# Late modulation vectors as float32 products on TensorE, and six of sixteen gate blocks issued beside the attention's first four query blocks

## Chip, cores and metric

One core of one Trainium2 chip. The metric is the device time of one execution in microseconds (us). The engines are named TensorE (PE in the rows; PEld is its weight load), VectorE (DVE), ScalarE (ACT), GpSimd (POOL) and SyncE (SP). L1035 is line 1035 of the kernel.

## The reference, cut to what matters

The reference is one layer of a hybrid block over 1024 tokens of width 1024. What bears on this change:

```python
mod_x = silu(c) @ w_mod + b_mod              # (1, 6*1024), float32
sh1, sc1, g1, sh2, sc2, g2 = split(mod_x, 6)
hx = layer_norm(x) * (1 + sc1) + sh1
q, k, v, u_hy, gate_x = split(hx @ w_in)     # gate_x has 2048 columns
att = window_attention(q, k, v, k_ctx, v_ctx, sink)
hy = hyena(u_hy, ...)                        # short convolution, then two long ones
g_att, g_hy = split(sigmoid(gate_x), 2)
y = (g_att * (att @ w_ba) + g_hy * (hy @ w_bh)) @ w_o
x_mid = layer_norm(ALPHA * x + g1 * y, ln1_g, ln1_b)
h = layer_norm(x_mid) * (1 + sc2) + sh2
out = layer_norm(ALPHA * x_mid + g2 * moe(h), ln2_g, ln2_b)
```

The first two modulation vectors (sh1, sc1) are needed at the start. The other four, the late ones, are needed after the attention: g1 for the output projection, sh2 and sc2 for the second norm, g2 in the experts.

## The kernel before, in words

The kernel runs in stages: the Hyena filters and the normed input (to about 230 us), the two long convolutions with the projections beside them (230 to 634 us), the attention's query blocks 0 to 3 (634 to 745), blocks 4 to 7 with the first half of the merge beside them (745 to 853), the rest of the merge and the output projection, and from about 1000 us the experts, whose weights stream from memory to the end.

Every projection of the normed input (`proj`, products on L812) handles 128 output columns as a block: a weight block of 1024x128 is loaded on SP's queue (tile `wr`), split into two float16 parts by ScalarE (`wh`, L791) and VectorE (`wl`, L799), and multiplied in 2 halves of 512 tokens by 24 products each. A gate block (`gate(j)`, j from 0 to 15) passes the result through a sigmoid on ScalarE (L841) into a tile `t` and stores it to DRAM (`Gd[j]`) from ScalarE's queue; the merge loads it back. The first eight gate blocks belong to the attention's branch, the last eight to the Hyena's.

The long convolution (`hyena(hf, o, z)`) runs four times, for two halves of the channels and two orders. Each run transposes on TensorE, transforms by products (L899, then the inverse on L922), and does radix-8 butterflies on VectorE (L722, L747, L748, L763, L906 to L909, tile `bf`); it ends with z products on VectorE (L924, L926).

Late modulation (`mod_late`) makes each late vector on VectorE: for each of eight chunks of 128 input rows it loads 128x1024 of `w_mod` on ScalarE's queue (L1034) and does one multiply-add over 128x1024 into an accumulator (L1035). Products with a column of ones then sum over the partitions (16 for g2 on L1039, two halves for each of the others on L1047). The tile size t4 (five buffers) is shared by these loads, the accumulator, uconv's outputs and the gates' results.

Order: the code is generators that yield, and `mix(M, (F, k))` issues k steps of F for each step of M. Issue order sets the priority, `hp` raises it (the hyena's by 1000 or 1500, the weight splits and the projections' copies out of PSUM by 3000); a scheduler then lists the instructions of each engine by its own estimate of time, and each engine runs its list in order. Before, all sixteen gate blocks are issued beside the hyena and drained (`GD=1`), and then the attention begins. PSUM has three buffers `mm` (projections, attention scores for the maximum, merge), three `ff` (the transforms, attention scores for the exponential) and two `tp` (transposes, modulation, attention output).

The attention (`attn`, L975 to L1010) computes scores for the row maximum (L975, L976; the maximum on L977 and L978), scores again in the other orientation (L991 to L994), two exponentials on ScalarE (L996, L997), and the product with V (L1004 to L1006). After block 3 the space of the normed input and of the projections is given to the merge: the branch weights (`wb_load`, L1062 load, L1063 split, tile `big`) go there.

Of the kernel before, what the change touches and what calls it, by code (L numbers as in the profile page):

```python
# [13 lines left out]
F32 = mybir.dt.float32  # L14
# [4 lines left out]
AF = mybir.ActivationFunctionType  # L19
ALU = mybir.AluOpType  # L20
# [74 lines left out]
class Moe:  # L95
# [144 lines left out]
    def prep_(s,C,p,pos,M,res,G0=None,late=None):  # L240

        nc,wk,ps=s.nc,s.wk,s.ps
        n=-(-C//128); chunks=[]; G={}; st={}
        def one():

            for i in range(min(n,2) if late is None else 1): hot(i)
# [9 lines left out]
        def gather(i):  # L256
# [13 lines left out]
            else:  # L270
# [4 lines left out]
                late.append(f); s.order.append(csi.ins)  # L275
            g=G[i]=G0[i] if G0 is not None else wk.tile([128,2,D],F16,name="g%d"%p,bufs=2)
            nc.gpsimd.indirect_dma_start(out=g[:cs].rearrange("p a d -> p (a d)"),out_offset=None,in_=s.rows,in_offset=bass.IndirectOffsetOnAxis(ap=gi[:cs,:1],axis=0))  # L277
            chunks.append((c0,cs,si,gc))
        def tr(i):

            if i==0:
                st['x']=wk.tile([128,2,8,PMAX[p]],F16,name="xT%d"%p,bufs=1); res.append((st['x'],chunks))
            c0=i*128; cs=min(128,C-c0); g=G.pop(i)
            for q in range(2):
# [153 lines left out]
    def experts(s,only=None):  # L438
# [14 lines left out]
        s.tail=[]; ready=[[],[]]; preps=[None,None]; run=[None,None]; done=[0,0]  # L453
        def nextprep(l,G=None,late=None):
            preps[l]=s.prep(seq[l][done[l]],l,ready[l],G,late) if done[l]<len(seq[l]) else None
            if preps[l] and G is None: preps[l][0].append(lambda r=seq[l][done[l]]: s.brs.__setitem__(s.regs[r],s.bias_load(s.regs[r]())))
            done[l]+=1
# [480 lines left out]
class PhaseA2(PhaseA):  # L938
# [86 lines left out]
    def mod_late(s):  # L1025

        nc,A=s.nc,s.A
        for n,nm in ((5,'g2'),(2,'g1'),(3,'sh2'),(4,'sc2')):
            acc=s.t4()
            nc.gpsimd.memset(acc,0.0)  # L1030
            if nm!='g2': nc.scalar.dma_start(acc[0:1],A['b_mod'][0:1,n*1024:(n+1)*1024])
            for k in range(8):
                w=s.t4()
                nc.scalar.dma_start(w,A['w_mod'][k*128:(k+1)*128,n*1024:(n+1)*1024])  # L1034
                (nc.gpsimd if s.poolm else nc.vector).scalar_tensor_tensor(acc,w,s.S[:,0,k:k+1],acc,op0=ALU.mult,op1=ALU.add)  # L1035
                yield
            if nm=='g2':
                p=s.ptp()[:,:8]
                for j in range(8): nc.tensor.matmul(p[:,j:j+1],acc[:,j*128:(j+1)*128],s.ones32[:,0:1],start=True,stop=True)  # L1039
                s.g2c=s.mcp.tile([128,8],F32,name="g2c"); s.g2s=s.mcp.tile([128,8],F32,name="g2s")  # L1040
                nc.vector.tensor_tensor(s.g2c,p,s.cols[:,88:96],op=ALU.add)
                nc.vector.tensor_scalar(s.g2s,s.g2c,2.**-10/ALPHA,None,op0=ALU.mult)
                nc.vector.tensor_scalar(s.g2c,s.g2c,1.0/ALPHA,None,op0=ALU.mult)
            else:
                r=acc
                for h in range(2):
                    p=s.ptp()[0:1]; nc.tensor.matmul(p,s.ones32[:,0:1],acc[:,h*512:(h+1)*512],start=True,stop=True)  # L1047
                    sc,bi={'g1':(1.0,0.0),'sc2':(1.0,1.0),'sh2':(1.0,0.0)}[nm]
                    nc.scalar.activation(r[0:1,h*512:(h+1)*512],p,AF.Copy,scale=sc,bias=bi)
                nc.sync.dma_start(s.rowD[n-2:n-1],r[0:1])  # L1050
            yield
    poolm=False

# [139 lines left out]
        c+=k  # L1193
        while c>=1: next(M,None); c-=1
SK=2
GD=1
HP0,HP1=1000,1500
def skew(gens,lag):

# [5 lines left out]
def drain(*gs):  # L1205
    for g in gs:
        for _ in g: pass
def chain(*gs):
    for g in gs: yield from g
# [7 lines left out]
def build(nc,tc,A,out,dbg=None,nexp=32):  # L1217
    with ExitStack() as es:
# [3 lines left out]
        with ExitStack() as ea:  # L1222
# [47 lines left out]
            F=chain(*[a.uconv(8+c,a.zt[c]) for c in range(4)],*[a.uconv(j) for j in range(4)])  # L1270
# [7 lines left out]
            drain(F)  # L1278
            nc.sync.dma_start(a.dft2,dq('idft')); a.idft=a.dft2
            F=chain(*[a.uconv(4+j) for j in range(4)],a.vproj(),*[a.qk(wq,j) for j in (4,0,1,2,3)])  # L1280
            G=chain(F,*[a.gate(j) for j in range(16)])
            ML=a.mod_late()
            mix(hp(chain(a.hyena(0,0,a.zt[0:2]),a.hyena(1,0,a.zt[2:4])),HP0),(G,K2),(ML,KM))
            drain(F)
# [2 lines left out]
            a.nq2=1; a.attn_k(w0); a.attn_q(0)  # L1287
            mix(hp(chain(a.hyena(0,1,a.zt[0:2]),a.hyena(1,1,a.zt[2:4])),HP1),(G,K2G),(ML,KM))
            drain(ML)
            if GD: drain(G)  # L1290
            eK.close()
            wa=eA.enter_context(E("wa","right"))
            a.aT=[wa.tile([128,4,1024],F16,name="aT%d"%q) for q in range(2)]
# [75 lines left out]
```

## Time and profile before

| | us |
|---|---|
| median of 3 runs | 2408.18 |
| lowest and highest | 2398.25, 2410.37 |
| the profiled execution, own time | 2412.69 |
| its span | 2410.9 |
| TensorE busy | 2199.2 |
| VectorE busy | 2053.8 |
| ScalarE busy | 1399.8 |
| GpSimd busy | 287.6 |

The profile is of one execution. Busy time is the union of the instructions' durations on an engine; a product's duration covers its way through the array, so that products that follow each other overlap, and the distance of their starts tells what one costs. The granted clock is TensorE's, as a share of full speed.

### The profile page before, as it was taken

What the parts mean: (1) busy time and instruction counts of PE and PEld (TensorE: products, weight loads), DVE (VectorE), ACT (ScalarE), POOL (GpSimd) and SP (SyncE); (2) the same over time, 40 slices, a digit from 0 to 9 for tenths busy, and PEclk for the clock granted to TensorE, in tenths of its full rate; (3) what the DMA queues carried; (4) which work ended last, traced back from release to release, by engine and by line L of the source; (5) the groups of instructions that cost most, each with busy time, mean ns of one, the idle gap of its engine ahead of it and who ended that gap; (6) DMA issues with size and microseconds to landing.
All of it is one profiled execution on the core that took longest, in us unless ns stands there. A gap on an engine that the chain in (4) does not pass through costs nothing.

```text
span 2410.9 us, 59658 instructions
## 1 busy us (share of the span) xinstructions
PE 2199.2 (91%) x24732; PEld 1659.4 (69%) x24753; DVE 2053.8 (85%) x3767; ACT 1399.8 (58%) x2069; POOL 287.6 (12%) x176
## 2 busy tenths in 40 slices
PE   6899989999898999669999999998989999999991
PEld 4566565545454544346666778997989999999991
DVE  6776898798768858969989999988999999999985
ACT  3522335222236411356877778886878878788881
POOL 0000001000000000002031311212030221211110
PEclk9899999999779999779999999999999999999995
DMA  9424644555314233288999999999999999999984
GB/s 300 127 97 166 194 149 132 170 181 169 94 18 144 84 121 139 89 275 280 337 316 303 328 323 348 356 352 320 333 332 350 359 351 354 351 356 368 360 273 159
DMA packets 520011, 594.17 MB, mean 246 GB/s; under 512 B 16708, under 2 KB 472332, under 8 KB 519350
## 3 DMA queue, kind: packets, MB, share of 16 engines
q1 hardware_dynamic: 493048, 508.27, 62.6%
q0 software_dynamic: 13152, 43.69, 7.1%
q10 hardware_dynamic: 13534, 38.35, 4.7%
q8 instruction: 195, 3.19, 0.5%
q14 instruction: 82, 0.67, 0.1%
HBM read 532.95 MB, written 57.29 MB: 245 GB/s over the span
## 4 chain that ended last, share of the span: by engine, by line
PE 72%; DVE 15%; DMA 6%; ACT 3%; issue 3%; SPq 1%; DVEq 0%; ACTq 0%; POOLq 0%
PE acc L347 38%; PE mm L812 10%; DVE wl L317 4%; PE mm L1080 4%; PE mm L1121 3%; DVE bf L722 2%; PE ff L704 2%; DMA raw<-in_exp_w 2%; PE acc L344 2%; PE mm L975 2%; PE yt L433 1%; ACT wh L315 1%; DMA g<-rows,gi 1%; PE ff L899 1%; PE mm L572 1%
## 5 line engine op out<-in xcount | busy, mean ns | idle before, releaser
L317 DVE SCALAR_TENSOR_TENSOR wl<-raw,wh 128x1024 f16<-128x1024 f32 x768 | 906.0, 1215 | 56.2 <-ACT wh L315 52.7
L315 ACT ACTIVATE wh<-raw 128x1024 f16<-128x1024 f32 x768 | 769.9, 1050 | 181.7 <-PE acc L347 92.6
L347 PEld LDWEIGHTS <-wh 128*128 128x128 f16 x9984 | 778.2, 99 | 85.8 <-issue 12.9
L347 PE MATMUL acc<-xT,wh 128*128 128x80 f16 (+18 forms) x6656 | 717.3, 235 | 2.9 <-ACT wh L315 1.2
L347 PE MATMUL acc<-xT,wl 128*128 128x112 f16 (+19 forms) x3328 | 638.0, 235 | 2.3 <-DVE wl L317 2.3
L347 PEld LDWEIGHTS <-wl 128*128 128x128 f16 x4992 | 488.9, 98 | 45.7 <-issue 7.2
L347 PE MATMUL acc<-ah,wh 128*128 128x112 f16 (+19 forms) x1664 | 323.9, 236 | 6.0 <-ACT yT L421 3.0
L812 PE MATMUL mm<-hx,wh 128*128 128x512 f16 (+1 forms) x1072 | 322.7, 378 | 6.7 <-DVE hx L635 5.9
L347 PE MATMUL acc<-al,wh 128*128 128x112 f16 (+19 forms) x1664 | 323.3, 236 | 3.7 <-DVE al L403 3.7
L347 PE MATMUL acc<-ah,wl 128*128 128x112 f16 (+19 forms) x1664 | 322.3, 236 | 0.0
L812 PE MATMUL mm<-hx,wl 128*128 128x512 f16 x536 | 202.8, 378 | 0.0
L277 POOL DMA_INDIRECT g<-rows,gi x44 | 139.2, 3165 | 459.5 <-DVE tf L266 435.4
L436 POOL DMA_INDIRECT accD<-yr,si x49 | 115.9, 2366 | 617.2 <-ACT yr L435 383.3
L812 PEld LDWEIGHTS <-wh 128*128 128x128 f16 x1072 | 105.2, 98 | 118.8 <-issue 2.9
L722 DVE TENSOR_TENSOR bf<-bf 128x256 f32<-128x256 f32 (+1 forms) x272 | 131.2, 541 | 0.3
L421 ACT ACTIVATE yT<-acc,bc,g2s 128x112 f32<-128x112 f32 (+19 forms) x208 | 98.8, 484 | 25.7 <-PE acc L347 25.6
L812 PEld LDWEIGHTS <-wl 128*128 128x128 f16 x536 | 52.5, 98 | 66.4 <-issue 8.5
L394 DVE TENSOR_SCALAR sl<-acc,bc 128x112 f32<-128x112 f32 (+19 forms) x208 | 75.3, 377 | 14.8 <-PE acc L347 14.5
L344 PEld LDWEIGHTS <-wl 128*128 128x128 f16 x1152 | 78.2, 98 | 11.3 <-issue 8.8
L393 DVE TENSOR_SCALAR sg<-acc,bc 128x112 f32<-128x112 f32 (+19 forms) x208 | 75.3, 377 | 12.4 <-PE acc L347 12.2
L344 PEld LDWEIGHTS <-wh 128*128 128x128 f16 x1152 | 79.6, 102 | 4.0 <-DVE yT L420 2.1
L791 ACT ACTIVATE wh<-wr 128x1024 f16<-128x1024 f32 (+1 forms) x49 | 38.4, 813 | 72.0 <-PE mm L812 51.7
(379 smaller groups left out, 3409.0 us busy)
## 6 DMA issues: line engine op xcount, KB each, us to landing
raw<-in_exp_w SPq DMA_DIRECT2D x384, 1024.0 KB
wr<-in_w_in SPq DMA_DIRECT2D x34, 512.0 KB
t<-in_w_mod ACTq DMA_DIRECT2D x32, 512.0 KB
bf<-in_dec SPq DMA_DIRECT2D x32, 256.0 KB
Hd<-bf ACTq DMA_DIRECT2D x32, 256.0 KB
bf<-Hd SPq DMA_DIRECT2D x32, 256.0 KB
Gd<-t ACTq DMA_DIRECT2D x16, 512.0 KB
gt<-Gd SPq DMA_DIRECT2D x32, 256.0 KB
```

The lines of the kernel that those rows point to most:

```text
L277: nc.gpsimd.indirect_dma_start(out=g[:cs].rearrange("p a d -> p (a d)"),out_offset=None,in_=s.rows,in_offset=bass.IndirectOffsetOnAxis(ap= ...
L315: else: nc.scalar.activation(wh[:,o],raw[:,o],AF.Copy,scale=sc)
L317: else: nc.vector.scalar_tensor_tensor(wl[:,o],raw[:,o],64.0,wh[:,o],op0=ALU.mult,op1=ALU.subtract)
L344: nc.tensor.matmul(ps_,wh,x[k],start=k==0,stop=False); nc.tensor.matmul(ps_[:,0],wl,x[k][:,0],start=False,stop=k==7)
L347: nc.tensor.matmul(ps_,a,b,start=n==0,stop=n==23); n+=1
L393: nc.vector.tensor_scalar(g[:,j],pg[:,j],bc[:,f:f+1],448.0,op0=ALU.add,op1=ALU.min)
L394: nc.vector.tensor_scalar(l[:,j],pl[:,j],bc[:,8+f:9+f],512.0,op0=ALU.add,op1=ALU.min)
L421: nc.scalar.activation(y,py,AF.Identity,bias=bc[:,16+m:17+m],scale=s.g2s[:,m:m+1])
L436: st=nc.gpsimd.indirect_dma_start(out=s.accD,out_offset=bass.IndirectOffsetOnAxis(ap=si[:cs,:1],axis=0),in_=yr[:cs],in_offset=None,compute ...
L722: (nc.gpsimd if pool and s.usepool else nc.vector).tensor_tensor(o,a,b,op=op)
L812: nc.tensor.matmul(p,w[a][:,k,:],s.hx[b][:,k,o],start=i==0,stop=i==23); i+=1
L1080: nc.tensor.matmul(p,w[a_][:,k,m*128:(m+1)*128],X[x][:,k,o] if b==0 else X[x][:,k,:],start=n==0,stop=n==11); n+=1
```

## The change

`mod_late` now loads `w_mod` by blocks of 128 output columns (all 1024 input rows, as 8 chunks beside each other in one tile) and sums over the inputs on TensorE in float32: eight products accumulate in one PSUM tile. For g1, sh2 and sc2 the conditioning column is the weight operand and 128 columns of `w_mod` move; for g2 the block of `w_mod` is the weight operand and the column moves, so that the result lies along the partitions. One short VectorE instruction adds the bias. The sum over partitions, the memsets, and ScalarE's copies of the rows are gone. And gate blocks 10 to 15 are no longer issued beside the hyena: after the others are drained, they become the side work of the attention's blocks 0 to 3, three steps for each step of the attention (a gate has six steps, and there are twelve attention steps).

```diff
         for n,nm in ((5,'g2'),(2,'g1'),(3,'sh2'),(4,'sc2')):
-            acc=s.t4()
-            nc.gpsimd.memset(acc,0.0)
-            if nm!='g2': nc.scalar.dma_start(acc[0:1],A['b_mod'][0:1,n*1024:(n+1)*1024])
-            for k in range(8):
-                w=s.t4()
-                nc.scalar.dma_start(w,A['w_mod'][k*128:(k+1)*128,n*1024:(n+1)*1024])
-                (nc.gpsimd if s.poolm else nc.vector).scalar_tensor_tensor(acc,w,s.S[:,0,k:k+1],acc,op0=ALU.mult,op1=ALU.add)
+            row=None if nm=='g2' else s.t4()
+            if row is not None: nc.scalar.dma_start(row[0:1],A['b_mod'][0:1,n*1024:(n+1)*1024])
+            if row is None: s.g2c=s.mcp.tile([128,8],F32,name="g2c"); s.g2s=s.mcp.tile([128,8],F32,name="g2s")
+            for j in range(8):
+                w=s.t4().rearrange("p (k f) -> p k f",k=8); c=n*1024+j*128
+                nc.scalar.dma_start(w,A['w_mod'][:,c:c+128].rearrange("(k p) f -> p k f",p=128))
+                if row is None:
+                    p=s.ptp()[:,0:1]
+                    for k in range(8): nc.tensor.matmul(p,w[:,k,:],s.S[:,0,k:k+1],start=k==0,stop=k==7)
+                    nc.vector.tensor_tensor(s.g2c[:,j:j+1],p,s.cols[:,88+j:89+j],op=ALU.add)
+                else:
+                    p=s.ptp()[0:1,:128]; r=row[0:1,j*128:(j+1)*128]
+                    for k in range(8): nc.tensor.matmul(p,s.S[:,0,k:k+1],w[:,k,:],start=k==0,stop=k==7)
+                    nc.vector.scalar_tensor_tensor(r,p,1.0 if nm=='sc2' else 0.0,r,op0=ALU.add,op1=ALU.add)
                 yield
-            if nm=='g2':
-                p=s.ptp()[:,:8]
-                for j in range(8): nc.tensor.matmul(p[:,j:j+1],acc[:,j*128:(j+1)*128],s.ones32[:,0:1],start=True,stop=True)
...
-            G=chain(F,*[a.gate(j) for j in range(16)])
+            G=chain(F,*[a.gate(j) for j in range(10)])
...
             drain(ML)
-            if GD: drain(G)
+            drain(G); G=chain(*[a.gate(j) for j in range(10,16)])
```

The line that follows in both kernels is `mix(chain(*[a.attn_blk(wt,i) for i in range(4)]),(G,K3))` with K3 = 3; before, G was empty by then.

## Rows read from the trace of the kernel before

**Rows 1.** Windows by stage: length; busy us (instructions) by engine; granted clock; DMA share; GB/s.
```profile
230.00:340.00 110.00, 102.00 (x650) 63.18 (x649) 97.95 (x169) 35.98 (x71) 6.37 (x21) 0.95 0.59 192
340.00:440.00 100.00, 100.00 (x509) 54.06 (x508) 92.61 (x164) 46.60 (x81) 13.90 (x23) 1.00 0.42 132
440.00:530.00 90.00, 88.47 (x435) 48.52 (x434) 70.95 (x120) 19.25 (x33) 0.94 (x1) 0.98 0.58 177
530.00:570.00 40.00, 40.00 (x218) 25.22 (x216) 31.96 (x46) 10.10 (x14) 0.00 (x0) 1.00 0.55 176
570.00:634.00 64.00, 55.22 (x282) 29.71 (x281) 60.68 (x114) 9.95 (x14) 0.00 (x0) 0.93 0.46 141
634.00:745.00 111.00, 100.20 (x843) 53.86 (x855) 73.17 (x155) 51.30 (x104) 0.00 (x0) 0.76 0.22 54
745.00:853.00 108.00, 104.63 (x902) 55.45 (x908) 94.99 (x169) 54.71 (x98) 0.00 (x0) 0.97 0.32 105
```
**Rows 2.** Groups of instructions by line, 230 to 640 us: busy us, mean ns | idle before.
```profile
L1035 DVE SCALAR_TENSOR_TENSOR t<-t,S,t 128x1024 f32<-128x1024 f32 x32 | 40.9, 1278 | 17.6 <-DMA t<-in_w_mod 17.6
L799 DVE SCALAR_TENSOR_TENSOR wl<-wr,wh 128x1024 f16<-128x1024 f32 x21 | 25.6, 1217 | 2.3 <-ACT wh L791 2.3
```
**Rows 3.** One line's instructions, L1041: duration ns min/median/max, first and last start.
```profile
L1041 DVE TENSOR_TENSOR g2c<-tp,cols x1: 155/155/155, 318.8 to 318.8; 128x8 f32<-128x8 f32 x1
```
**Rows 4.** VectorE in order of time, 624 to 629 us: start, us, instruction.
```profile
626.93 1.01 DVE L977 TENSOR_REDUCE mx<-mm 128x1 f32<-128x384 f32 x2
627.86 0.68 DVE L978 TENSOR_REDUCE mx<-mm 128x4 f32<-128x512 f32 x1
628.46 1.21 DVE L926 TENSOR_TENSOR z<-z,so 128x1024 f32<-128x1024 f32 x1
```
**Rows 5.** Chain of work that ended last, 380 to 430 us: start, us, what.
```profile
382.90 37.12 PE mm L812 x172
420.02 1.81 PE tp L1047 x4
```
**Rows 6.** TensorE in order of time, 310 to 318 us.
```profile
312.67 3.51 PE L1039 MATMUL tp<-ones,t 128*128 128x1 f32 x16
```
**Rows 7.** TensorE in order of time, 20 to 24 us.
```profile
21.21 1.91 PE L572 MATMUL mm<-hx,S 128*2 128x128 f32 x16
```
**Rows 8.** VectorE's waits, 230 to 634 us: us in total, times, longest.
```profile
DVE t L1035 <- DMA t<-in_w_mod: 17.6, 9, 4.4
DVE bf L722 <- ACT bf L729: 14.4, 8, 4.2
DVE z L924 <- PE ff L922: 6.9, 4, 3.2
```
**Rows 9.** Windows of 10 us in the two stages of the attention.
```profile
640.00:650.00 10.00, 10.00 (x43) 3.92 (x43) 6.47 (x14) 4.38 (x10) 0.00 (x0) 0.50 0.25 51
800.00:810.00 10.00, 9.95 (x107) 5.92 (x109) 9.49 (x16) 4.91 (x9) 0.00 (x0) 1.00 0.12 42
```
**Rows 10.** Window of the second stage, merge products of L1080 alone: TensorE and weight loads.
```profile
745.00:853.00 108.00, 47.44 (x192) 19.01 (x192) 0.97 0.32 105
```
**Rows 11.** ScalarE in order of time, 402 to 416 us.
```profile
406.55 0.58 ACT L866 ACTIVATE qx<-mm 128x512 f32<-128x512 f32 x1
407.15 1.28 ACT L841 ACT_TABLE_LOAD   x1
408.62 0.60 ACT L841 ACTIVATE t<-mm 128x512 f32<-128x512 f32 x1 [0.19 <-PE mm L812]
```
**Rows 12.** ScalarE in order of time, 434 to 437 us.
```profile
436.22 1.06 ACT L791 ACTIVATE wh<-wr 128x1024 f16<-128x1024 f32 x1 [1.29 <-PE mm L812]
```
**Rows 13.** SP's queue in order of time, 605 to 760 us.
```profile
611.88 0.81 SPq L1062 DMA_DIRECT2D big<-in_w_branch_attn  x2
...
734.99 1.47 SPq L1062 DMA_DIRECT2D big<-in_w_branch_attn  x2
```
**Rows 14.** TensorE in order of time, 607 to 612 us.
```profile
608.18 0.38 PE L812 MATMUL mm<-hx,wl 128*128 128x512 f16 x1
608.49 0.28 PE L975 MATMUL mm<-K,Q 64*128 64x128 f16 x2
```
**Rows 15.** ScalarE in order of time, 725 to 750 us.
```profile
742.04 1.06 ACT L1063 ACTIVATE w_branch_attnh<-big 128x1024 f16<-128x1024 f32 x1 [1.07 <-DMA big<-in_w_branch_attn]
```

More of the change, by code (lines that the diff above doesn't have):

```diff
@@ L1037, in mod_late @@
-            if nm=='g2':
-                p=s.ptp()[:,:8]
-                for j in range(8): nc.tensor.matmul(p[:,j:j+1],acc[:,j*128:(j+1)*128],s.ones32[:,0:1],start=True,stop=True)
-                s.g2c=s.mcp.tile([128,8],F32,name="g2c"); s.g2s=s.mcp.tile([128,8],F32,name="g2s")
-                nc.vector.tensor_tensor(s.g2c,p,s.cols[:,88:96],op=ALU.add)
+            row=None if nm=='g2' else s.t4()
+            if row is not None: nc.scalar.dma_start(row[0:1],A['b_mod'][0:1,n*1024:(n+1)*1024])
@@ L1042, in mod_late @@
+            if row is None:
                 nc.vector.tensor_scalar(s.g2s,s.g2c,2.**-10/ALPHA,None,op0=ALU.mult)
                 nc.vector.tensor_scalar(s.g2c,s.g2c,1.0/ALPHA,None,op0=ALU.mult)
[L1044 to L1050, printed above, removed]
+            else: nc.sync.dma_start(s.rowD[n-2:n-1],row[0:1])
@@ L1195 @@
 SK=2
-GD=1
 HP0,HP1=1000,1500
```

## The prediction

> **What bounds the kernel now.** I read the 40-slice overview first, and then cut the part that the change touches into stages [rows 1]. From 230 to 634 us the long convolution ("hyena") runs on VectorE, and the projections (uconv, qk, gates) fill TensorE beside it; from 634 to 745 us the first four query blocks of the attention run alone; from 745 to 853 us the last four run beside the first half of the merge. In the first stretch both engines are nearly full: TensorE has 102 + 100 + 88.5 + 40 + 55.2 = 385.7 us busy of 404, VectorE 98 + 92.6 + 71 + 32 + 60.7 = 354.2. In the last 64 us VectorE has 60.7 and TensorE 55.2, so this stretch ends on VectorE. The attention alone is another picture: TensorE is marked busy for 100.2 of 111 us, but with a mean granted clock of 0.76, VectorE for 73.2, ScalarE for 51.3. Nothing after 853 us is touched.
>
> **Late modulation, VectorE.** The change takes away 32 multiply-adds over 128x1024, 40.9 us in all [rows 2]. It adds 32 short additions out of PSUM: eight over one column and 24 over 128 columns of one partition. No row has the second form. The same kind over 8 columns takes 0.155 us [rows 3], a PSUM read over 512 columns 0.68 us [rows 4]; on the line between them 128 columns cost 0.28 us, which I take. 24 x 0.28 + 8 x 0.155 = 8 us (5 to 18 at the two ends). The six moved gate blocks take 6 x 1.217 = 7.3 us of weight splitting with them [rows 2]. VectorE's load up to the end of the hyena falls by 40.9 + 7.3 - 8 = 40 us.
>
> **Late modulation, TensorE.** Taken away: 12 products of 0.45 us (four in 1.81, [rows 5]), 5.4 us, and the 16 of g2, 3.5 us [rows 6]. Added for g1, sh2, sc2: 3 x 8 x 8 = 192 products with one column of weights and 128 float32 columns moving. The early modulation has two columns of weights and the same 128: 16 in 1.91 us, of which 0.27 is the tail of the last, so (1.91 - 0.27)/15 = 0.109 us each [rows 7], and 192 x 0.109 = 20.9 us. Added for g2: 64 products with 128x128 float32 weights and one column; the 16 of before took 0.21 us each [rows 6], 64 x 0.21 = 13.4 us; priced like the 192 it would be 7. I take 10.
>
> Here a rule speaks against the change: the Trainium skill (FP8 and Floating Point Precision, TensorE Precision Notes) says that true float32 takes four passes through the array. An estimate by it is four times the 16-bit column time, 0.21 us for 128 columns, 41 us instead of 20.9. The row has 0.109 us, half of that, so I keep the row.
>
> **The gates that move.** A gate block is 48 products of 512 columns; the chain shows 172 in 37.12 us, 0.216 each [rows 5], 10.4 a block, 62.2 for six. TensorE's load up to the end of the hyena becomes 385.7 - 62.2 - 5.4 - 3.5 + 20.9 + 10 = 345.5 us. VectorE, with its idle time unchanged at 404 - 354.2 = 49.8, ends 40 us sooner, at 594, 364 us after 230. That is more than 345.5, so VectorE sets this end and TensorE has 18.5 us free. Term one: -40 us. With the products move six weight loads of 512 KB on SP's queue and six stores of the results on ScalarE's; the DMA engines are busy for 0.22 in 634:745 [rows 1], so I cost them at nothing: the merge wants the first moved gate only for its sixth group of products (second branch, third block of columns).
>
> **What is left of the idle time.** 17.6 us of VectorE's idle time are waits of the removed multiply-adds for their loads, nine of them, up to 4.4 us long [rows 8]. I let this cancel: the same loads now hold TensorE, in whose order the hyena's transforms stand behind the waiting product, and VectorE waits for those. At the ends it is -17.6 (all gone) or +17.6 (as long on TensorE with no other work in reach). The 32 loads stay on ScalarE's queue, 512 KB each, with shorter runs; I cost them at no difference, as their issue stays behind ScalarE's work and that engine is busy for at most 47 of 100 us [rows 1]. The cover would be gone if a load landed later than its product's turn, which is the +17.6. GpSimd's four memsets go, off every chain.
>
> **Attention, blocks 0 to 3.** The granted clock shows what the filler is worth. In 640:650 the engine is marked busy throughout with 43 matmuls at 0.50, the lower of its levels (1.2 GHz); with the merge's products beside the attention, in 800:810, it has 107 at 1.00 (2.4 GHz) [rows 9]. At full clock the first four blocks need 100.2 x 0.76 = 76 us. The other way: in 745:853, TensorE's 104.6 us less 192 merge products [rows 10] x 0.216 = 41.4 leave 63.2 us, at 0.97 61, for 902 - 192 = 710 attention matmuls; for 843 that makes 73. I take 75. With the gates, 75 + 62.2 = 137 us; filled as well as that stage (104.6/108 = 0.97) it takes 141 us instead of 111. Term two: +30 us. Lower end: 25 (full engine and 73); upper end 45 (a fill of 0.88).
>
> **ScalarE in that stretch.** It gets 12 sigmoids of 0.60 us, 7.2, six weight copies of 1.06, 6.4 [rows 11, 12], and, what is new, a change of function table whenever a sigmoid stands between exponentials. Before, all sigmoids came first, with one load of 1.28 us [rows 11]. At worst there are 24 loads, 30.8 us. 51.3 + 7.2 + 6.4 + 30.8 = 96 of 141 us, so the sum holds them hidden beside the gates' products; without cover they cost up to 31.
>
> The Trainium skill (ScalarE: Activation LUTs, What ACT_TABLE_LOAD costs) adds a drain of about 1.38 us to each load, 2.66 in all; an estimate for 24 is 64 us, and ScalarE would have 129 of 141. The row does not show the drain: the load begins 0.02 us after the copy before it ends, and the sigmoid 0.19 us after the load, waiting for TensorE [rows 11]. I keep 1.28.
>
> **Two small terms.** First, the merge's weights. Their first two loads were issued at 611.88 us [rows 13], 3.3 us after the last gate product ended [rows 14]: they wait for the space that the projections read. Now this space is free only when the last gate is done, near the end of block 3. The second pair of before shows the lag, issued at 734.99 [rows 13] and copied by ScalarE, which had waited for it, at 742.04 [rows 15], 7 us. Block 4 covers part of it: 0 to 7, I take +3. Second, TensorE's 18.5 free us before the hyena's end: a gate could run there, but as soon as the gates issued earlier were done, the first attention scores took the three product buffers (608.49), and the VectorE reduction that frees one came at 626.93 [rows 14, 4]. So 0 to 18.5; I take -7.
>
> **Sum.** -40 + 30 + 3 - 7 = -14 us. The profiled execution took 2412.7 us, so 2398.7; it lies 4.5 above the median of the three runs (2408.2), and on that scale the forecast is 2394 us. Its own range, with the ends of the short additions, g2 and the fill, is 2382 to 2409.
>
> **Rivals.** (A) The waits for the loads really go, since a product needs one engine less and gives its buffer back sooner: -14 - 17.6 = -32 us, 2376. For it: nine waits in the rows, and VectorE's waits for the transforms (14.4 and 6.9 us, [rows 8]), which fewer products in TensorE's order would shorten; against: the same loads and buffers. (B) The removed additions only filled VectorE's holes. The hyena has priority, and in 440:570 VectorE is busy for 103 of 130 us, so much of the work was free, and the hyena ends when its own chain ends. If only 10 of the 40 us arrive, the sum is -10 + 30 + 3 - 7 = +16, 2424: slower, since the six gates still lengthen the attention by 30. It decides as soon as less than 26 us arrive. Against it: in 340:440 and 570:634 VectorE has hardly a hole, 92.6 of 100 and 60.7 of 64 us busy [rows 1]. (C) The table loads stand on the chain: every exponential waits for them, the gates on TensorE run dry, and -14 + 31 = +17, 2425. For it: ScalarE's copies feed the products directly. Against: 45 us of slack in the stretch. (D) TensorE takes over the nine load waits as they are, in front of the hyena: -14 + 17.6 = +4, 2412, no change.
>
> **How the numbers follow.** About 12 us (0.5%) is what a measurement of this kernel can tell from no change. Forecast 0.38, a little over half of it beyond -12; A 0.24; B 0.16; C 0.10; D 0.12. Faster: 0.21 + 0.24 = 0.45. Same: 0.17 + 0.11, and 0.06 from the mild ends of B and C, 0.34. Slower: 0.21. The range, 2364 to 2424, takes in A with 12 us to spare and reaches B.
>
> **What would show it.** The hyena's last product on z (line 926) should start near 590 us instead of 628.46 [rows 4], with VectorE still full in the last 60 us; the mean granted clock of the first four query blocks should rise from 0.76 to above 0.95, and that stage last about 140 us. The 192 products should stand 0.11 us apart. Ends above 615 for the hyena make B right; waits of TensorE for the modulation weights of over 10 us make D; waits of exponentials behind table loads C. The forecast is wrong if the hyena shortens by less than 26 us or the attention stage passes 155 us.

## The result and the profile after

The changed kernel takes 2468.3 us (median of four runs, 2460.9 to 2471.9), the kernel before 2403.9 beside it: a ratio of 1.0255 [1.0216, 1.0294]. The forecast was 2394 us. The profiled execution took 2460.9 us, its span is 2459.2, 48.3 more than before; the medians lie 64 apart, since the profiled execution of before (2412.7) is slower than the four runs beside it, and that of after the fastest of its own. Two executions of 5605 and 5874 us, one of before and one of e6, are left out of the ratios below as slow ones.

Four marks divide the span, and they will serve for the experiments too: the start of the hyena's last product on z (L926 in every kernel), of the last gate product with `wh` (L812), and of ScalarE's copy of the result of attention blocks 3 and 7 (L1021), with which a block is all but done. Each is read from one execution. The hyena's first transpose (L893), which stands ahead of all that the change and the experiments touch, starts at 162.9 us in before and between 157.5 and 164.6 in the sixteen traces, so a few us between two marks say nothing. The difference at block 7 is 46.2 of the 48.3 us, so nearly all of it lies in the stretch that the prediction cut into stages.

| | hyena's last | gates' last | block 3 | block 7 |
|---|---|---|---|---|
| before | 628.5 | 608.0 | 744.4 | 854.0 |
| after | 623.4 | 767.3 | 776.1 | 900.2 |
| difference | -5.1 | | +31.7 | +46.2 |

The windows of after, by stage, with the columns of [rows 1]:

```profile
230.00:340.00 110.00, 110.00 (x637) 70.55 (x635) 94.83 (x174) 31.19 (x56) 4.62 (x19) 0.95 0.58 183
340.00:440.00 100.00, 100.00 (x698) 63.43 (x697) 92.50 (x185) 45.45 (x87) 11.78 (x20) 1.00 0.35 108
440.00:530.00 90.00, 87.96 (x480) 46.18 (x479) 61.10 (x113) 17.83 (x26) 1.22 (x2) 0.98 0.60 181
530.00:570.00 40.00, 40.00 (x207) 21.59 (x206) 20.30 (x38) 10.02 (x17) 0.00 (x0) 1.00 0.38 118
570.00:629.00 59.00, 42.97 (x274) 28.43 (x271) 48.28 (x94) 4.95 (x6) 0.00 (x0) 0.86 0.52 148
629.00:780.00 151.00, 142.32 (x1109) 72.84 (x1109) 73.00 (x143) 85.73 (x130) 0.00 (x0) 0.93 0.22 62
780.00:900.00 120.00, 113.45 (x936) 58.14 (x935) 103.54 (x185) 62.67 (x111) 0.00 (x0) 0.93 0.35 115
```

Read the first five windows by engine. VectorE's busy time up to the hyena's end fell from 354.2 us [rows 1] to 94.8 + 92.5 + 61.1 + 20.3 + 48.3 = 317.0, so the 37 us that the change takes from it are gone. But its idle time rose from 404 - 354.2 = 49.8 us to 399 - 317.0 = 82.0, by 32, and that leaves the 5 us at the mark. TensorE's hardly fell, 385.7 to 380.9, though six gate blocks (62.2 us) left. It is full from 230 to 570, at the end of which VectorE has 20.3 of 40 us; after that VectorE has 48.3 of 59 and TensorE 43.0. The two engines are bound one after the other instead of together.

What filled TensorE stands in the groups of instructions by line, 230 to 629 us (busy us, mean ns | idle before):

```profile
L812 PE MATMUL mm<-hx,wh 128*128 128x512 f16 (+1 forms) x704 | 213.6, 382 | 0.0
L1041 PE MATMUL tp<-t,S 128*1 128x128 f32 x384 | 48.0, 277 | 4.7 <-DMA t<-in_w_mod 4.6
L1037 PE MATMUL tp<-S,t 128*128 128x1 f32 x128 | 15.3, 251 | 0.0
```

The code writes 192 products at L1041 and 64 at L1037. The trace has 384 and 128: each float32 product is two TensorE instructions. One group in order of time (start, us) is 16 instructions for the eight products of one block of columns:

```profile
333.18 1.69 PE L1041 MATMUL tp<-t,S 128*1 128x128 f32 x14
335.86 0.38 PE L1041 MATMUL tp<-t,S 128*1 128x128 f32 x2
```

[rows 7] show the same: "x16" there was eight products with both halves, not sixteen. The instruction costs what the prediction took for a product, 0.109 us; 384 x 0.109 is 41.9 us. (The 48.0 us of busy time hold the tails of the groups too.)

How a full TensorE reaches VectorE shows in VectorE's waits, 230 to 620 us (total, times, longest):

```profile
DVE bf L722 <- ACT bf L729: 24.5, 8, 4.3
DVE wl L799 <- ACT wh L791: 20.3, 4, 11.1
DVE z L924 <- PE ff L922: 12.5, 5, 4.2
DVE t L1042 <- PE tp L1041: 10.6, 6, 2.6
```

The waits for modulation loads, 17.6 us [rows 8], are gone. In their place VectorE waits for weight copies of ScalarE (20.3 us against 2.3, [rows 2]), and ScalarE, ahead of such a copy, had waited for gate products of L812. One such pair, ScalarE's copy and VectorE's split behind it:

```profile
519.55 1.06 ACT L791 ACTIVATE wh<-wr 128x1024 f16<-128x1024 f32 x1 [4.37 <-PE mm L812]
520.64 1.23 DVE L799 SCALAR_TENSOR_TENSOR wl<-wr,wh 128x1024 f16<-128x1024 f32 x1 [7.61 <-ACT wh L791]
```

In the attention's first four blocks the new thing is on ScalarE. Its groups, 629 to 780 us:

```profile
L841 ACT ACT_TABLE_LOAD x12 | 15.4, 1283 | 0.2
L996 ACT ACT_TABLE_LOAD x7 | 9.0, 1283 | 0.5 <-ACT t L841 0.4
L983 ACT ACT_TABLE_LOAD x4 | 5.1, 1283 | 3.1 <-DVE m L982 2.6 <-ACT t L841 0.4
```

23 table loads, 29.5 us. One sigmoid among exponentials, in order of time:

```profile
647.19 1.28 ACT L841 ACT_TABLE_LOAD   x1
648.48 0.60 ACT L841 ACTIVATE t<-mm 128x512 f32<-128x512 f32 x1
649.10 1.28 ACT L996 ACT_TABLE_LOAD   x1
...
650.39 0.60 ACT L996 ACTIVATE ph<-ff 128x512 f16<-128x512 f32 x1
```

From 647.19 to 650.39 the engine gives the attention nothing: 3.2 us around a sigmoid of 0.6.

### The profile page after: what moved, and what is told of

It reads as the page before. It is cut to its first block, busy times and chain, and to the rows that moved or that the text cites. A ratio compares the mean times of both kernels' runs of the same rounds, so it can differ in the third digit from the quotient of the medians.

```text
span 2459.2 us, 60637 instructions
## 1 busy us (share of the span) xinstructions
PE 2244.2 (91%) x25236; PEld 1692.9 (69%) x25237; DVE 2024.2 (82%) x3766; ACT 1430.9 (58%) x2087; POOL 291.3 (12%) x172
## 5 line engine op out<-in xcount | busy, mean ns | idle before, releaser
L315 ACT ACTIVATE wh<-raw 128x1024 f16<-128x1024 f32 x768 | 769.5, 1050 | 182.6 <-PE acc L347 92.7
L812 PE MATMUL mm<-hx,wh 128*128 128x512 f16 (+1 forms) x1072 | 330.1, 385 | 6.0 <-DVE hx L635 4.4
L812 PE MATMUL mm<-hx,wl 128*128 128x512 f16 x536 | 205.7, 384 | 0.0
L436 POOL DMA_INDIRECT accD<-yr,si x49 | 122.2, 2495 | 608.6 <-ACT yr L435 360.6
L812 PEld LDWEIGHTS <-wh 128*128 128x128 f16 x1072 | 106.4, 100 | 118.5 <-issue 11.1
L722 DVE TENSOR_TENSOR bf<-bf 128x256 f32<-128x256 f32 (+1 forms) x272 | 130.6, 540 | 0.3
L812 PEld LDWEIGHTS <-wl 128*128 128x128 f16 x536 | 53.3, 99 | 66.2 <-issue 11.4
```

Of the source, the lines that this page charges most:

```text
L315: else: nc.scalar.activation(wh[:,o],raw[:,o],AF.Copy,scale=sc)
L436: st=nc.gpsimd.indirect_dma_start(out=s.accD,out_offset=bass.IndirectOffsetOnAxis(ap=si[:cs,:1],axis=0),in_=yr[:cs],in_offset=None,compute ...
L722: (nc.gpsimd if pool and s.usepool else nc.vector).tensor_tensor(o,a,b,op=op)
L812: nc.tensor.matmul(p,w[a][:,k,:],s.hx[b][:,k,o],start=i==0,stop=i==23); i+=1
```

## The experiments

In e3, e4, e9 and e10 the later parts of the kernel work on other values, so only the marks ahead of them are read. All marks together:

| | hyena's last | gates' last | block 3 | block 7 | ratio to before |
|---|---|---|---|---|---|
| e1, products alone | 614.7 | 662.7 | 769.5 | 877.8 | 1.0102 [1.0063, 1.0141] |
| e2, gates alone | 614.7 | 759.2 | 768.0 | 889.9 | 1.0147 [1.0090, 1.0204] |
| e3, no sigmoid beside attention | 626.9 | 755.2 | 764.5 | 885.5 | |
| e4, half the products | 612.6 | 759.6 | 768.4 | 889.5 | |
| e5, e2 with gates twice as fast | 614.9 | 710.1 | 777.4 | 884.6 | 1.0173 [1.0120, 1.0226] |
| e6, e2 with tanh | 612.3 | 740.6 | 749.7 | 870.0 | 1.0108 [1.0043, 1.0173] |
| e7, GpSimd alone | 670.1 | 681.2 | 786.4 | 892.5 | 1.0230 [1.0179, 1.0281] |
| e8, ScalarE and GpSimd | 655.6 | 667.6 | 782.2 | 892.4 | 1.0174 [1.0125, 1.0224] |
| e9, e1 with half the products | 604.0 | 637.0 | 747.6 | 854.3 | |
| e10, multiply-adds cut short | 607.3 | 621.9 | 730.7 | 839.2 | |
| e11, tanh and two gates moved | 617.6 | 653.5 | 736.4 | 846.0 | 1.0023 [0.9985, 1.0061] |
| e12, products beside attention | 590.6 | 600.8 | 772.0 | 880.5 | 1.0201 [1.0153, 1.0248] |
| e13, multiply-adds beside attention | 589.0 | 599.2 | 742.4 | 854.0 | 1.0065 [1.0033, 1.0097] |
| e14, two vectors beside attention | 611.9 | 595.5 | 735.3 | 844.2 | 0.9998 [0.9966, 1.0029] |

**The two parts, each alone.** e1 is the changed kernel with all 16 gates beside the hyena; e2 is the kernel before with six gates moved.

```diff
 # e1, against the changed kernel
-            G=chain(F,*[a.gate(j) for j in range(10)])
+            G=chain(F,*[a.gate(j) for j in range(16)])
-            drain(G); G=chain(*[a.gate(j) for j in range(10,16)])
+            drain(G)
 # e2, against the kernel before
-            G=chain(F,*[a.gate(j) for j in range(16)])
+            G=chain(F,*[a.gate(j) for j in range(10)])
-            if GD: drain(G)
+            drain(G); G=chain(*[a.gate(j) for j in range(10,16)])
```

> Only the modulation part of the change; all sixteen gate blocks stay beside the hyena. Load theory: TensorE is the bound up to the end of the attention, and each float32 product is two instructions of 0.109 us, so 192 + 64 products add 48 us to it (48 of L1041 busy less the sums taken away); the end of the hyena moves from 629 to 660 or later, the attention's first four blocks stay at about 111 us, and the time is 30 to 48 us above before. Attention theory: the loss comes from the gates beside the attention (table loads, product buffers), so this kernel is within 12 us of before or faster by up to 30.

> Only the gates part: blocks 10 to 15 beside the attention's blocks 0 to 3, modulation on VectorE as before. Load theory: TensorE's work is that of before and the attention's clock rises, so the time is 0 to 20 us below before. Attention theory: the 23 table loads and the shared buffers lengthen the attention by more than the hyena gives back, and the time is 25 to 50 us above before.

Each part alone is a loss at block 7's end, 23.8 and 35.9 us, and together they cost 46.2. Of e1's load theory the price came out (28.7 us between the medians, where it had 30 to 48), but not the place: it had the hyena end at 660 or later, and that is where the gates end. In e2 the attention theory's range holds (38.2 us between the medians). In e1 TensorE is the bound: windows with the columns of [rows 1].

```profile
570.00:615.00 45.00, 45.00 (x268) 25.67 (x267) 40.95 (x77) 7.47 (x10) 0.00 (x0) 1.00 0.53 162
615.00:660.00 45.00, 42.04 (x217) 20.07 (x216) 6.67 (x9) 7.12 (x10) 0.00 (x0) 1.00 0.59 152
```

After the hyena's end, 45 us hold nothing but the gates that had no room (VectorE 6.7 us busy). In e2 it is the reverse:

```profile
530.00:570.00 40.00, 20.14 (x100) 15.58 (x100) 38.67 (x61) 5.39 (x8) 0.00 (x0) 0.80 0.44 152
570.00:615.00 45.00, 14.96 (x80) 12.76 (x81) 41.69 (x82) 1.06 (x1) 0.00 (x0) 0.57 0.16 45
```

VectorE is full and TensorE has 20 + 30 = 50 us free. Before, the gates had filled these 50 us, and cost the hyena's end at most the 13.8 us that e2 gains there; beside the attention the 62 us of products cost 37.4 us in blocks 0 to 3 and 12.3 in blocks 4 to 7. TensorE's longest waits of e2, 230 to 640 us, show the hole:

```profile
PE ff L922 <- DVE bf L722: 37.8, 2, 36.0
```

**The price of the products.** Half of the products left out, in the changed kernel (e4) and in e1 (e9).

```diff
 # L1041; g2's line, L1037, in the same way
-    for k in range(8): nc.tensor.matmul(p,s.S[:,0,k:k+1],w[:,k,:],start=k==0,stop=k==7)
+    for k in range(4): nc.tensor.matmul(p,s.S[:,0,k:k+1],w[:,k,:],start=k==0,stop=k==3)
```

> The changed kernel with half of the late modulation's products left out (the sums take 4 of the 8 chunks of input rows; loads and everything else stay). Load theory: half of L1041 and L1037, 384 + 128 instructions, some 29 us of TensorE, goes, and the time falls by 20 to 29 us. Attention theory: these products ran beside other work, and the time falls by less than 8 us.

> The modulation-only kernel with half of the float32 products left out (4 of 8 chunks of input rows), so its output and its expert stage differ; it is read by its marks before the experts. In that kernel TensorE is full up to the last gate at 662.7 us and block 7 of the attention ends at 877.8. Load theory: 256 instructions fewer, 27 us of TensorE, bring the last gate to 636 to 646 and block 7's end to 851 to 861. Rival (the products run beside other work, and their waits for loads or for the two buffers cost, not their time): both marks move by less than 10 us.

The groups of e9, 230 to 664 us:

```profile
L1041 PE MATMUL tp<-t,S 128*1 128x128 f32 x192 | 25.6, 273 | 2.7 <-DMA t<-in_w_mod 2.5 <-ACT sm L894 0.2
L1037 PE MATMUL tp<-S,t 128*128 128x1 f32 x64 | 7.5, 242 | 0.0
```

96 products are 192 instructions: two each, without a count to be argued. With 33.1 us of them, close to the 30.9 that the prediction had set, the hyena ends 10.7 us sooner than in e1, the gates 25.7, block 7 23.5, at 854.3: the mark of before. Gates and block 7 lie in the load theory's ranges. So the second instruction of each product is worth what e1 lost.

In the changed kernel it is worth less. In e4 the hyena gains 10.8 us and block 7 10.7, between the two theories. With the products near the price that the forecast had set, the hyena ends at 612.6 instead of the forecast's 590, and block 7 at 889.5; e2, with the whole modulation on VectorE, has 614.7 and 889.9, which is no difference. So even at the lower price the exchange would have gained nothing here. The window of e4 at the end of the hyena:

```profile
570.00:615.00 45.00, 22.13 (x119) 16.02 (x118) 34.88 (x65) 2.12 (x2) 0.00 (x0) 0.70 0.32 93
```

TensorE, busy for 291.6 of the 300 us from 230 to 530 in e4, has its free time here.

**Where the relief of VectorE goes.** e10 keeps the loads and the order of before and cuts 28 of the 32 multiply-adds to one column; nothing goes to TensorE.

```diff
-                (nc.gpsimd if s.poolm else nc.vector).scalar_tensor_tensor(acc,w,s.S[:,0,k:k+1],acc,op0=ALU.mult,op1=ALU.add)
+                c=slice(0,1024) if k==0 else slice(k,k+1)
+                nc.vector.scalar_tensor_tensor(acc[:,c],w[:,c],s.S[:,0,k:k+1],acc[:,c],op0=ALU.mult,op1=ALU.add)
```

> The kernel before with 28 of the 32 multiply-adds cut to one column (the sums miss 7 of 8 chunks, so output and expert stage differ; read by its marks). VectorE loses 34 us, TensorE gets nothing, GpSimd does nothing. The prediction's term one said that the hyena's end moves by nearly all of what leaves VectorE: from 628.5 to 595 to 605, and block 7's end from 854 to 820 to 835. Room theory: TensorE is full to 608 before, so the gates still end at 600 or later, and the attention starts no more than 8 to 18 us sooner; block 7 ends at 836 to 846.

The hyena ends 21.2 us sooner, of some 34 us taken from VectorE (607.3; term one had 595 to 605), the last gate 13.9 later, and block 7 14.8 sooner, as the room theory had it. Half of the 13 us that don't arrive are waits for the loads that are still there: they grew from 17.6 us [rows 8] to 24.0.

```profile
DVE t L1036 <- DMA t<-in_w_mod: 24.0, 10, 9.8
```

e12 and e13 take the modulation out of the hyena and put it beside attention blocks 0 to 3, as products on TensorE (e12, from e1) or as the multiply-adds of before on VectorE (e13).

```diff
 # e12 and e13 alike, the lines that change the place of the modulation (ML)
-            mix(hp(chain(a.hyena(0,0,a.zt[0:2]),a.hyena(1,0,a.zt[2:4])),HP0),(G,K2),(ML,KM))
+            mix(hp(chain(a.hyena(0,0,a.zt[0:2]),a.hyena(1,0,a.zt[2:4])),HP0),(G,K2))
...
-            mix(hp(chain(a.hyena(0,1,a.zt[0:2]),a.hyena(1,1,a.zt[2:4])),HP1),(G,K2G),(ML,KM))
-            drain(ML)
+            mix(hp(chain(a.hyena(0,1,a.zt[0:2]),a.hyena(1,1,a.zt[2:4])),HP1),(G,K2G))
...
-            mix(chain(*[a.attn_blk(wt,i) for i in range(4)]),(G,K3))
-            drain(G)
+            mix(chain(*[a.attn_blk(wt,i) for i in range(4)]),(ML,4.0))
+            drain(ML)
```

> All sixteen gates beside the hyena as before, and the late modulation as float32 products beside the attention's blocks 0 to 3 instead (the stage that has a granted clock of 0.76). Room theory: the hyena and its gates lose VectorE's 41 us and 9 us of TensorE and end 8 to 18 us sooner, the attention gets 57 us of TensorE work at the price that the gates with tanh showed there (22 us for 62): the time lies between -8 and +14 us of before. Rival: as side work of the attention the products cost their full 57 us less the gain of the clock, and the time is 25 us or more above before.

> The late modulation on VectorE as before, but issued beside the attention's blocks 0 to 3 instead of beside the hyena; gates all beside the hyena. In the kernel with the float32 products at this place the hyena ended 38 us sooner (590.6) and the attention's first stage grew by 65 us. Engine theory: the products' TensorE time made that growth; without them the hyena still ends at 588 to 598, the stage lasts 116 to 140 us, as VectorE has 73 + 41 us of work in it, and block 7 ends at 825 to 850: the time is 5 to 25 us below before. Place theory: the late loads and the shared buffers beside the attention made it; the stage lasts 150 us or more here too, and the time is 10 us or more above before.

The hyena ends 37.9 and 39.5 us sooner, with all 16 gates still beside it. That this is near the 40 us of term one is in part luck: these runs take away the loads too, for which VectorE had waited 17.6 us, so 58 us leave it and 38 to 39.5 arrive. It needs a VectorE that is relieved and a TensorE that is not loaded in exchange. But the attention gives it back: from the hyena's last product to block 3 takes 181 us in e12 and 153 in e13, against 116 before. Why the products cost 28 us more than the multiply-adds shows in the windows of e12 and of e13:

```profile
595.00:755.00 160.00, 153.55 (x1326) 99.46 (x1335) 74.78 (x171) 43.85 (x88) 0.00 (x0) 0.88 0.53 144
```

```profile
600.00:660.00 60.00, 45.66 (x339) 23.99 (x338) 48.62 (x84) 22.05 (x43) 1.90 (x2) 0.71 0.66 199
660.00:740.00 80.00, 67.61 (x564) 32.98 (x565) 60.59 (x110) 29.90 (x61) 0.95 (x1) 0.85 0.48 143
```

In e12 TensorE is full (153.6 of 160), and the rival of its expectation came true. In e13 neither engine is. By its expectation's own signs that is the place theory (150 us or more, and 10 us or more above before: the ratio's 0.65% is 16 us); whether the late loads, the shared buffers or the attention's own order sets the pace there was not tested. At block 7 e13 stands where before stood (854.0); the marks don't hold what the time loses behind it.

**The table loads.** e3 replaces the sigmoid of the six moved gates by a plain copy; e6 computes it as tanh of half the argument, in e2.

```diff
 # e3
+            with s.hp(): nc.scalar.activation(g[:,h*512:(h+1)*512],p,AF.Sigmoid if j<10 else AF.Copy,scale=2.**-6)
 # e6, beside e2's lines
+            with s.hp(): nc.scalar.activation(g[:,h*512:(h+1)*512],p,AF.Tanh,scale=2.**-7)
...
+                if b==0: nc.vector.scalar_tensor_tensor(mg,gt,1.0,p,op0=ALU.add,op1=ALU.mult)
...
+            nc.scalar.activation(s.mT[0][:,m,o],mg,AF.Copy,scale=0.5)
```

> The changed kernel with a copy in place of the sigmoid in gate blocks 10 to 15 (these gates are left without their function), so that no table load falls between exponentials: 23 loads of 1.28 us, 29.5 us, leave ScalarE. Load theory: they stood beside TensorE's work, the time falls by less than 8 us. Attention theory: it falls by 20 to 30 us.

> The gates-only kernel with the sigmoid computed as (1 + tanh(x/2))/2: tanh on ScalarE, the addition and the product in one VectorE instruction of the merge, the half in the copy behind it. The Trainium skill (ScalarE: Activation LUTs, Table sets) lists tanh in the set of the exponential. If that holds here, 0 or 1 table loads remain in the attention instead of 23 and, by the step from 900 to 885 us that the kernel without sigmoids showed, the time falls by 12 to 16 us against gates-only's 2448. Rival: the loads are beside TensorE's work in this kernel, less than 6 us.

Without loads the four blocks take 137.6 us (e3) and 137.4 (e6) from the hyena's last product, against 152.7 in the changed kernel and 153.3 in e2. The window of e6, with the columns of [rows 1]:

```profile
612.00:750.00 138.00, 136.92 (x1112) 72.66 (x1119) 75.67 (x148) 54.30 (x105) 0.00 (x0) 1.00 0.28 71
```

TensorE is filled to 0.99 at the upper clock level (granted 1.00), where the changed kernel had 0.94 at 0.93. So 15 to 16 us of the 29.5 us of loads stood on the chain. At block 7 e3 is 14.7 us ahead of the changed kernel and e6 19.9 ahead of e2; e6's median is 18 us below e2's, but they ran beside different runs of before, and by the ratios it is some 9 us, with intervals that overlap. In e6 no table load stands in this stretch. The Trainium skill (ScalarE: Activation LUTs, Table sets: the hidden batching unit) lists tanh in the exponential's set; the trace agrees with it.

**The wait for the merge's weights.** e5 issues the gates twice as fast beside the attention (K3 = 6 for 3), so that the last is done at 710 instead of 759 us.

> The gates-only kernel with K3 = 6 instead of 3: the six gates are issued within the first six of the twelve attention steps, so the space that the merge's first weights wait for is free before block 3 ends. Lag theory: the 122 us of blocks 4 to 7 (before: 110) fall back to 108 to 113, and the time falls by 8 to 13 us against the gates-only kernel's 2448, the first four blocks staying at about 153 us. Rival: the longer second stage comes from its clock or its own order, and it stays at 120 us or more.

SP's queue (start of the issue of the first two weight loads), first of the changed kernel, then of e5:

```profile
772.15 0.82 SPq L1059 DMA_DIRECT2D big<-in_w_branch_attn  x2
```

```profile
714.16 0.82 SPq L1062 DMA_DIRECT2D big<-in_w_branch_attn  x2
```

The issue follows the mark of the last gate by 4.9 and 4.1 us; before it was 611.88 [rows 13] - 608.0 = 3.9. With the early load, blocks 4 to 7 take 107.2 us instead of e2's 121.9, as the lag theory had it; before it was 109.6. So a late last gate costs 12 to 15 us there, not 3. But blocks 0 to 3, which that theory left at 153 us, grow by 9 in e5: block 7 comes 5.3 us sooner, and the time is not better than e2's (1.0173 against 1.0147).

**Other engines for the modulation.** From before: multiply and add on GpSimd (e7), or the product on ScalarE and the addition on GpSimd (e8).

```diff
 # e7, in place of the multiply-add
+                nc.gpsimd.tensor_scalar(w,w,s.S[:,0,k:k+1],0.0,op0=ALU.mult,op1=ALU.add)
+                nc.gpsimd.tensor_tensor(acc,acc,w,op=ALU.add)
 # e8, in place of the multiply-add
+                nc.scalar.activation(w,w,AF.Copy,scale=s.S[:,0,k:k+1])
+                nc.gpsimd.tensor_tensor(acc,acc,w,op=ALU.add)
```

> The kernel before with the late modulation's 32 multiply-adds on GpSimd, as a multiplication and an addition each; nothing else changed. VectorE loses 41 us and TensorE gets nothing. Room theory: both engines then have at most 386 us to do between 230 and the end of the hyena, the end comes 8 to 18 us sooner, and the time falls by as much, to 2390 to 2400. Rival (the hyena's own chain sets its end, and the multiply-adds filled holes): no change, within 6 us; slower if GpSimd's stores (Sd, QD, KD) queue behind its arithmetic.

> As the GpSimd kernel, but with the multiplication on ScalarE (1.05 us each, 34 us in all) and only the addition on GpSimd. Room theory: as there, 8 to 18 us below before, unless ScalarE's copies out of PSUM come late for TensorE. Rival: no change, within 6 us, or slower by ScalarE's 34 us where it stands in front of the copies.

The hyena ends 41.6 and 27.1 us later, though VectorE does less; neither theory had that. VectorE's own instructions became longer: from 230 us to some 5 us past the mark it is busy for 393.7 us in e7 where before had 354.2, and idle for 51.3 where before had 49.8, so the longer instructions are the whole loss. In e8 it is busy for 369.7 and idle for 61.3: 15.5 us of the loss are longer instructions, 11.5 are waits. The means of e7, 230 to 670 us:

```profile
L722 DVE TENSOR_TENSOR bf<-bf 128x512 f32<-128x512 f32 x104 | 82.3, 824 | 0.2
L909 DVE TENSOR_TENSOR bf<-bf 128x256 f32<-128x256 f32 x64 | 37.5, 626 | 0.3
L722 DVE TENSOR_TENSOR bf<-ff,bf 128x512 f32<-128x512 f32 x34 | 23.4, 688 | 25.7 <-ACT bf L729 25.4
L924 DVE SCALAR_TENSOR_TENSOR z<-z,skip,ff 128x512 f32<-128x512 f32 x16 | 18.1, 1151 | 6.7 <-PE ff L922 6.7
```

and the same groups of before, 230 to 634 us:

```profile
L722 DVE TENSOR_TENSOR bf<-bf 128x512 f32<-128x512 f32 x104 | 67.7, 682 | 0.2
L722 DVE TENSOR_TENSOR bf<-ff,bf 128x512 f32<-128x512 f32 x36 | 24.7, 687 | 14.7 <-ACT bf L729 14.4
L909 DVE TENSOR_TENSOR bf<-bf 128x256 f32<-128x256 f32 x64 | 23.9, 416 | 0.1
L924 DVE SCALAR_TENSOR_TENSOR z<-z,skip,ff 128x512 f32<-128x512 f32 x16 | 18.0, 1150 | 6.9 <-PE ff L922 6.9
```

The means hide how. L909 by shortest, median and longest, in e7 and in before:

```profile
L909 DVE TENSOR_TENSOR bf<-bf x64: 409/414/2570, 287.1 to 645.4; 128x256 f32<-128x256 f32 x64
L909 DVE TENSOR_TENSOR bf<-bf x64: 409/416/426, 291.8 to 603.9; 128x256 f32<-128x256 f32 x64
```

Most of them take what they took, and single ones up to 2.2 us more. GpSimd's multiplications and additions take 2.37 and 2.54 us on average.

**Versions that might beat both.** e11 is before with tanh and only the last two gates moved; e14 is before with the multiply-adds of sh2 and sc2 alone beside the attention.

```diff
 # e11, beside e6's lines with tanh
+            G=chain(F,*[a.gate(j) for j in range(14)])
+            drain(G); G=chain(*[a.gate(j) for j in range(14,16)])
 # e14
+            ML=a.mod_late(); MA=islice(ML,18)
...
+            mix(chain(*[a.attn_blk(wt,i) for i in range(4)]),(ML,3.0))
```

> The kernel before with the sigmoid through tanh and gate blocks 14 and 15 beside the attention. Room theory: the last two gates (21 us of TensorE) stood in the 50 us that gates-only left free, the hyena ends 3 to 10 us sooner, the attention's first stage grows by 2 x 3.6 = 7 us, no table load is left, the space for the merge is free before block 2: the time is within 8 us of before. Rival: the attention's rise of the clock pays and the time falls by 12 us or more.

> As that kernel, with only sh2 and sc2 (half of the multiply-adds) beside the attention, and g2 and g1 beside the hyena. Engine theory: half the relief and half the price: the hyena ends at 605 to 615, the stage lasts 112 to 128 us, the time is 4 to 18 us below before. Place theory: the stage lasts 135 us or more, no gain.

At block 7's end they lie 8.0 and 9.8 us ahead of before, but neither can be told from it in time: 2410.9 us against 2405.9, 2404.7 against 2400.5. So e11 is where its room theory had it, and e14 has the hyena's end and the stage of its engine theory (611.9 and 123.4 us) without the gain. Part of the leads is no gain at all: the hyena's first transpose starts at 158.3 and 159.8 us, 4.6 and 3.1 ahead of before's 162.9, and nothing that these kernels change stands in front of it. Runs of the kernel before alone spread from 2394 to 2431 us, more than the gain looked for.

## Why the prediction was wrong

**The step that failed: term one, -40 us at the hyena's end, which came out as -5.** The sum put TensorE's load (345.5 us) below VectorE's 364 and so left VectorE's idle time unchanged at 49.8 us. The saving on VectorE was right (37 us less busy), but the idle time rose to 82.0: its waits for loads went, and waits for copies and sums that stand behind TensorE's products came in their place. With the tail of -7, which did not come either, this is 42 of the 60 us by which the marks miss the sum. Two things were wrong in it.

The first is the price: "Late modulation, TensorE", the 192 products at 0.109 us each. 16 instructions in [rows 7] were taken for 16 products and are eight; so are the 16 of [rows 6], which the description of the kernel before gives as 16 products too. The 192 cost 384 x 0.109 = 41.9 us, where the sum had 20.9. The Trainium skill's rule of four passes (FP8 and Floating Point Precision, TensorE Precision Notes), which the prediction weighed and set aside, gave 41 us for the 192; the 41.9 agree with it. For g2, 16 instructions hold TensorE for 1.70 us (263.69 to the next start at 265.39), 13.6 for 128, where the sum had 10. With these 24.6 us more the forecast's own TensorE load becomes 370, above the 364 us in which VectorE was to be done, and the sentence "VectorE sets this end and TensorE has 18.5 us free" falls. By e4 the price is 10.8 of the 35 us that term one missed; in e1, where the gates stay, it is the whole loss (e9).

The second is that the load was summed over 400 us, as if TensorE's time were worth the same everywhere in them. From 230 to 530 us TensorE was busy for 290.5 of 300 us in before [rows 1]. The gates that left had stood behind that: their sigmoids ran from 537 to 609 us. Of the 63.3 us of products that came, 44.1 ran before 530. So room was made at the end and needed at the beginning. What is more, with no gates beside them the last transforms (L922) ran at a granted clock of 0.50 from 600 to 610 us and 0.67 from 610 to 620, where before had 1.00 from 570 to 612. The other 24 us were missing in e4 as well. This part is read from the windows of before, after and e4; no run put the products at the end of the hyena, so it is not shown by a run of its own. e12 and e13 show that 38 to 39.5 us are there when the products stay away from the hyena.

In size this is near rival B (10 of 40 us arrive), but not in its mechanism: B said that the additions had only filled holes, and in e10, which takes away little else, 21.2 of some 34 us arrive.

**Term two, +30 us, was right but for its cover.** Measured are +36.8 (152.7 us from the hyena's last product to block 3, 115.9 before). Without table loads it is +21.5 (e6) and +21.7 (e3), at a fill of 0.99 where the forecast had counted on 0.97: less than the term. The 15 to 16 us between are rival C, held at a chance of 0.10: the loads do stand on the chain of exponentials. As the row had it, no drain shows behind a load; with the prediction's 1.28 us and the cover taken away, the price was within its bound of 31.

**The free tail.** "A gate could run there" (-7) failed: TensorE's free time in the last stretch stayed free, and in e2 it is 50 us. Before, the six gates had run there behind VectorE's work, at a price of at most 13.8 us (e2); the move made it 50.

**The merge's weights** cost 14.5 us in blocks 4 to 7 (124.1 us against 109.6), not 3. The lag of 7 us in [rows 15] was the wait of a second pair, whose first pair had long been there. Now the first pair is late too, and with it all of the merge's products; in e5, where it comes in time, these blocks take 107.2 us. But e5 pays 9 us of that in blocks 0 to 3, so the late gate is worth some 5 us at block 7 by this remedy.

**The waits for loads** went, as rival A had it (17.6 us), and TensorE's own waits for them are 4.6 us, so D was small; but VectorE's idle time as a whole grew by 32, so its other waits grew by some 50. The short additions took 0.27 us (0.28 was estimated).

By marks: -5.1 at the hyena's end, +36.8 in blocks 0 to 3, +14.5 in blocks 4 to 7, in all +46.2; the sum had -47 (terms one and the tail), +30 and +3. The prediction's own range of 2382 to 2409 does not follow from the ends that it names either: with 5 and 18 for the short additions and 25 and 45 for the fill, -14 - 3 - 5 and -14 + 10 + 15 on 2408 give 2386 to 2419, still far from the 2468. Two things stay open. The two parts together cost 13.5 us less than one by one, and both end the hyena later (623.4) than each alone (614.7): what does that was not tried. Against e1 the trace shows the place: both run alike up to a weight split of VectorE at 568.2 us (566.5 in e1), and the difference comes behind it, where TensorE of e1 is full at 1.00. And what is left of the leads of e11 and e14 at block 7 (some 3 and 7 us) is not seen in their medians; with one profile of each, and before's 2412.7 slower than its median, it may be chance.

## What to carry to other kernels

Before a row prices a new operation, tie its count to the code that made it: how many instructions of the trace does one call give? Sum the loads by stage, and not over a stretch of several: room that a change makes at the end of it doesn't serve work that is issued at its beginning. An engine may have idle time only in one place; work that runs there costs little, and moving it to a stage with another bound makes it a cost, even if that stage looks slack. A filler that needs its own function table, or whose end frees the space for the next stage's weights, brings both prices with it.

## What the runs showed of the hardware

A float32 product is two TensorE instructions, each of 0.109 us for 128 columns at the upper clock level (granted 1.00 from 330 to 340 us), where a 16-bit one takes 0.216 for 512 [rows 5].

While GpSimd did the modulation's arithmetic (e7, 253 to 639 us), VectorE's butterflies with both inputs in SBUF became longer on average (682 to 824 ns over 128x512, 416 to 626 over 128x256), but only where they met an instruction of that arithmetic. By the start and end of each in the trace, those of L909 in this stretch that overlap none, 46, take at most 426 ns; the 14 that do take 1378 on average and 2570 at most. The Trainium skill (SBUF — State Buffer, SBUF: two separate sides) states that GpSimd and VectorE share a pair of ports, which one of them holds for a whole instruction while the other waits, and that VectorE operations with two SBUF inputs are among those that contend; the rows agree. Instructions that read PSUM kept their time, but few of them met GpSimd's: four of L722 (690 ns on average) and none of L924.
